# Instance norm on one core: gamma first on the ScalarE queue, its columns and the Sqrt table made while the first unit lands

## The chip, the cores and the metric

The kernel runs on one core of a Trainium2 chip. The metric is the time on the device in microseconds (us), the median of several executions. The profile is of one execution; its span is some 1.7 us shorter than the time that is reported for the same execution (625.1 us against 626.8 us before the change).

## The reference

```python
def reference(x, gamma):              # x: 4 x 8 x 16 x 256 x 256 float32, gamma: 8 x 16
    mu = x.mean(axis=(3, 4), keepdims=True)
    var = ((x - mu) ** 2).mean(axis=(3, 4), keepdims=True)
    x_norm = (x - mu) / np.sqrt(var + 1e-5)
    out = x_norm * gamma[None, :, :, None, None]
```

There are 512 channels of 65,536 numbers. Each channel is normalised by its own mean and variance and multiplied by its gamma. The input is 134.2 MB and so is the output; every byte has to be read once and written once.

## The kernel before

The kernel takes 16 channels at a time, a *unit*: 8 partitions for each channel, 8192 numbers (32 KB) in each partition, 4 MB in all. There are 32 units and six slots in SBUF. All six slots are filled at the start, so six loads (about 25 MB) are queued before any arithmetic is done. A later load waits until the store from its slot has landed.

```python
    g_row = singles.tile([1, G * C], F32, name="g_row")
    for u in range(AHEAD):                                   # AHEAD = 6
        load(u, nc.scalar if u in (1, 3) else nc.sync)
        if u == 1:
            nc.sync.dma_start(out=g_row[:], in_=gv[None, :])
    ...
    for u in range(U):                                       # U = 32
        t = slots[u % AHEAD]
        nc.vector.reduce_sum(out=st[:, u, 0:1], in_=t[:], axis=AX.X)
        square = nc.scalar.activation(out=junk[:], in_=t[:], func=ACTF.Square, accum_out=st[:, u, 1:2])
        ...
        if u == 0:
            gamma_columns()          # 8 matmuls spread gamma over the partitions, between two copies
        ps = psum.tile([P, 2], F32, name="ps")
        nc.tensor.matmul(out=ps[:], lhsT=navg_w, rhs=st[:, u], start=True, stop=True)
        # nvar on VectorE, std (Sqrt) on ScalarE, rstd and scale on VectorE   (cut)
        nc.vector.tensor_scalar(out=t[:], in0=t[:], scalar1=ps[:, 0:1], scalar2=scale[:, u : u + 1],
                                op0=ALU.add, op1=ALU.mult)
        nc.scalar.dma_start(out=ov[u], in_=t[:])
        if u + AHEAD < U:
            load(u + AHEAD, nc.sync)
```

So loads go out on the SyncE queue, stores and two of the first loads on the ScalarE queue. In the records these are the DMA queues q1 and q10.

## Time and profile before

| What | Before | Read from |
|---|---|---|
| Time | 626.93 us (626.88 to 627.35) | median of all runs |
| Span of the profiled execution | 625.1 us | the page |
| Bytes moved | 268.46 MB, 429 GB/s over the span | the page |
| VectorE, ScalarE, TensorE busy | 71%, 38%, 3% | the page |
| Unit 0 landed, first store issued | 22.6 us, 43.1 us | the timeline |

These are lines of the page of the kernel before: busy time in us (share of the span) and number of instructions, then busy tenths in 40 equal slices for VectorE, ScalarE and the 16 DMA engines, then GB/s in each slice.

```profile
PE 21.4 (3%) x80; PEld 19.5 (3%) x80; DVE 442.9 (71%) x162; ACT 239.9 (38%) x98; POOL 1.3 (0%) x9
DVE  0569999999898767867668676686766877667710
ACT  0435555544444423444224442244432444323400
DMA  8999999999999999999999999999999999999998
GB/s 371 434 436 419 419 436 436 436 436 436 435 436 435 428 426 436 426 436 436 434 436 436 434 434 432 428 432 426 436 436 434 436 436 434 434 436 428 428 436 359
```

The DMA row has a 9 in every slice but the first and the last, and the rate stays near 436 GB/s. No engine that computes is in that position. The Trainium skill ("DMA: Bandwidth & Descriptors", section "Specifications") gives a fabric ceiling of 435 GB/s, and this trace runs at it.

The timeline of the kernel before, cut to the first unit. The columns are start and duration in us, engine, line, operation, what it writes and reads, and in brackets the idle time before it with what ended it.

```profile
1.72 1.28 ACT L103 ACT_TABLE_LOAD   x1 [1.72 <-PEq L148]
22.61 8.69 DVE L102 TENSOR_REDUCE st<-xt 128x1 f32<-128x8192 f32 x1 [22.61 <-DMA xt<-in_x_dram]
31.21 0.67 DVE L78 COPY g_rep<-g_row 1x1024 f32<-1x1024 f32 x1
32.02 3.54 PE L83 MATMUL g_ps<-one,g_rep 1*128 1x1 f32 x16 [32.02 <-DVE g_rep L78]
36.12 0.29 DVE L114 TENSOR_SCALAR nvar<-ps 128x1 f32<-128x1 f32 x1 [0.36 <-PE ps L113]
36.49 1.28 ACT L118 ACT_TABLE_LOAD   x1 [6.76 <-DVE nvar L114]
38.51 4.55 DVE L127 TENSOR_SCALAR xt<-xt,ps,scale 128x8192 f32<-128x8192 f32 x1
43.09 0.35 ACTq L131 DMA_DIRECT2D out_dram<-xt  x1
```

Between the end of the first row sum (31.3 us) and the first store (43.1 us) stand gamma's columns (the copy, 16 matmul passes of 3.54 us in all, a copy back) and a load of the Sqrt table (1.28 us), the second table load of the kernel. VectorE waits for both. This is what the change goes after.

### The profile page before, as it was taken

The numbers are of one execution on the slowest core, as the hardware profiler recorded it, in microseconds if no ns is written. First come the engines' busy times: TensorE is split into PE (matmuls) and PEld (weight loads), VectorE is DVE, ScalarE is ACT, GpSimd is POOL, SyncE is SP. The second block draws the span as 40 slices with busy tenths as digits, with TensorE's granted clock in tenths as the row PEclk, the third lists the DMA queues.
The fourth block names the chain that finished last, engine by engine and source line by source line (L and its number), as shares of the span: only waits on it lengthen the run. The fifth ranks groups of instructions, "written<-read, shape, count | busy, mean of one in ns | idle before, by whom it ended". The sixth has DMA issues, their size and how long they took to land.

```text
span 625.1 us, 628 instructions
## 1 busy us (share of the span) xinstructions
PE 21.4 (3%) x80; PEld 19.5 (3%) x80; DVE 442.9 (71%) x162; ACT 239.9 (38%) x98; POOL 1.3 (0%) x9
## 2 busy tenths in 40 slices
PE   0020000000000000000000000000000000000000
PEld 0020000000000000000000000000000000000000
DVE  0569999999898767867668676686766877667710
ACT  0435555544444423444224442244432444323400
POOL 0000000000000000000000000000000000000000
DMA  8999999999999999999999999999999999999998
GB/s 371 434 436 419 419 436 436 436 436 436 435 436 435 428 426 436 426 436 436 434 436 436 434 434 432 428 432 426 436 436 434 436 436 434 434 436 428 428 436 359
DMA packets 9220, 268.46 MB, mean 429 GB/s; under 512 B 1025, under 2 KB 1026, under 8 KB 1026
## 3 DMA queue, kind: packets, MB, share of 16 engines
q10 hardware_dynamic: 4896, 142.61, 52.8%
q1 hardware_dynamic: 4322, 125.83, 46.8%
q14 instruction: 2, 0.02, 0.0%
HBM read 134.22 MB, written 134.22 MB: 429 GB/s over the span
## 4 chain that ended last, share of the span: by engine, by line
DMA 62%; DVE 30%; PE 2%; issue 1%; ACT 1%; SPq 0%; ACTq 0%
DMA xt<-in_x_dram 55%; DVE st L102 24%; DMA out_dram<-xt 7%; DVE xt L127 5%; PE ps L113 2%; DVE nvar L114 1%; PE g_ps L83 1%; ACT std L118 0%; ACT L118 0%; DVE rstd L122 0%; DVE scale L124 0%; DVE g_rep L78 0%; SPq L48 0%; ACTq L118 0%
## 5 line engine op out<-in xcount | busy, mean ns | idle before, releaser
L102 DVE TENSOR_REDUCE st<-xt 128x1 f32<-128x8192 f32 x32 | 277.9, 8684 | 110.2 <-DMA xt<-in_x_dram 110.2
L103 ACT ACTIVATE junk<-xt 128x8192 uint8<-128x8192 f32 x32 | 224.9, 7030 | 266.1 <-DMA xt<-in_x_dram 212.1
L127 DVE TENSOR_SCALAR xt<-xt,ps,scale 128x8192 f32<-128x8192 f32 x32 | 145.6, 4550 | 1.2
L118 ACT ACTIVATE std<-nvar,eps_t 128x1 f32<-128x1 f32 x32 | 9.4, 295 | 76.0 <-DVE nvar L114 76.0
L113 PE MATMUL ps<-st,navg 128*128 128x2 f32 x64 | 17.9, 349 | 536.4 <-DVE st L102 536.4
L113 PEld LDWEIGHTS ps<-st,navg 128*128 128x128 f32 x64 | 16.0, 311 | 538.2 <-issue 538.2
L114 DVE TENSOR_SCALAR nvar<-ps 128x1 f32<-128x1 f32 x32 | 9.2, 286 | 23.4 <-PE ps L113 23.4
L122 DVE RECIPROCAL rstd<-std 128x1 f32<-128x1 f32 x32 | 5.2, 164 | 12.9 <-ACT std L118 12.9
L103 ACT ACTIVATION_READ_ACCUMULATOR junk<-xt 128x1 f32 x32 | 6.0, 186 | 0.0
L124 DVE TENSOR_TENSOR scale<-rstd,g_col 128x1 f32<-128x1 f32 x32 | 5.1, 159 | 1.1
L83 PE MATMUL g_ps<-one,g_rep 1*128 1x1 f32 x16 | 3.5, 346 | 32.0 <-DVE g_rep L78 32.0
L83 PEld LDWEIGHTS g_ps<-one,g_rep 1*128 1x128 f32 x16 | 3.5, 325 | 32.0 <-issue 32.0
L118 ACT ACT_TABLE_LOAD x1 | 1.3, 1283 | 6.8 <-DVE nvar L114 6.8
L89 DVE COPY g_col<-g_ps 128x8 f32<-128x8 f32 x1 | 0.2, 166 | 3.7 <-PE g_ps L83 3.7
L103 ACT ACT_TABLE_LOAD x1 | 1.3, 1283 | 1.7 <-PEq L148 1.7
L78 DVE COPY g_rep<-g_row 1x1024 f32<-1x1024 f32 x1 | 0.7, 670 | 0.0
L64 POOL TENSOR_SCALAR_AFFINE_SELECT navg<-navg 128x128 f32<-128x128 f32 x1 | 0.4, 405 | 0.1
L68 POOL TENSOR_SCALAR_AFFINE_SELECT navg<-navg 128x128 f32<-128x128 f32 x1 | 0.4, 399 | 0.1
L63 POOL MEMSET navg<- 128x128 f32 x1 | 0.2, 222 | 0.0
L148 POOL MEMSET const-bfloat16-1.0<- 128x1 bf16 x1 | 0.1, 102 | 0.0
L148 POOL MEMSET const-uint8-127<- 128x1 uint8 x1 | 0.1, 102 | 0.0
L148 POOL MEMSET const-float32-0.0<- 128x1 f32 x1 | 0.1, 99 | 0.3 <-issue 0.3
(3 smaller groups left out, 0.3 us busy)
## 6 DMA issues: line engine op xcount, KB each, us to landing
out_dram<-xt ACTq DMA_DIRECT2D x32, 4096.0 KB, 64.1
xt<-in_x_dram SPq DMA_DIRECT2D x30, 4096.0 KB, 29.0
xt<-in_x_dram ACTq DMA_DIRECT2D x2, 4096.0 KB, 31.4
g_row<-in_gamma_dram SPq DMA_DIRECT2D x1, 0.5 KB
```

The costliest lines, as they stand in the source:

```text
L64: nc.gpsimd.affine_select(out=navg[:], in_=navg[:], pattern=[[-S, K], [0, S]], compare_op=ALU.is_ge, fill=0.0, base=0, channel_multiplier=1,)
L68: nc.gpsimd.affine_select(out=navg[:], in_=navg[:], pattern=[[S, K], [0, S]], compare_op=ALU.is_ge, fill=0.0, base=S - 1, channel_multipli ...
L78: nc.vector.tensor_copy(out=g_rep[:], in_=g_row[:].rearrange("o (n k) -> o n k", n=NG).unsqueeze(3).to_broadcast([1, NG, K, S]),)
L83: nc.tensor.matmul(out=g_ps[:, n : n + 1], lhsT=g_rep[:, n].rearrange("o k s -> o (k s)"), rhs=one[:], start=True, stop=True,)
L102: nc.vector.reduce_sum(out=st[:, u, 0:1], in_=t[:], axis=AX.X)
L103: square = nc.scalar.activation(out=junk[:], in_=t[:], func=ACTF.Square, accum_out=st[:, u, 1:2],)
L113: nc.tensor.matmul(out=ps[:], lhsT=navg_w, rhs=st[:, u], start=True, stop=True)
L114: nc.vector.tensor_scalar(out=nvar[:, u : u + 1], in0=ps[:, 0:1], scalar1=ps[:, 0:1], scalar2=ps[:, 1:2], op0=ALU.mult, op1=ALU.add,)
L118: nc.scalar.activation(out=std[:, u : u + 1], in_=nvar[:, u : u + 1], func=ACTF.Sqrt, bias=eps_t[:], scale=-1.0,)
L122: nc.vector.reciprocal(out=rstd[:, u : u + 1], in_=std[:, u : u + 1])
L124: nc.vector.tensor_mul(out=scale[:, u : u + 1], in0=rstd[:, u : u + 1], in1=g_col[:, g : g + 1],)
L127: nc.vector.tensor_scalar(out=t[:], in0=t[:], scalar1=ps[:, 0:1], scalar2=scale[:, u : u + 1], op0=ALU.add, op1=ALU.mult,)
```

## The change

Gamma's 512 bytes become the first transfer of the ScalarE queue, and the columns are made before unit 0 lands. A root of a small constant tile, which nothing uses, makes ScalarE load the Sqrt table at the start.

```diff
     for u in range(AHEAD):
+        if u == 1:
+            nc.scalar.dma_start(out=g_row[:], in_=gv[None, :])
         load(u, nc.scalar if u in (1, 3) else nc.sync)
-        if u == 1:
-            nc.sync.dma_start(out=g_row[:], in_=gv[None, :])
...
+    root_eps = singles.tile([P, 1], F32, name="root_eps")
+    nc.scalar.activation(out=root_eps[:], in_=eps_t[:], func=ACTF.Sqrt)
...
-    def gamma_columns():
-        (copy to g_rep, 8 matmuls to g_ps, copy to g_col)
+    (the same copy, 8 matmuls and copy, at once)
...
-        if u == 0:
-            gamma_columns()
```

More of the change, by code (lines that the diff above doesn't have):

```diff
@@ L75 @@
     g_col = singles.tile([P, NG], F32, name="g_col")
-    def gamma_columns():
-        nc.vector.tensor_copy(
-            out=g_rep[:],
-            in_=g_row[:].rearrange("o (n k) -> o n k", n=NG).unsqueeze(3).to_broadcast([1, NG, K, S]),
-        )
-        for n in range(NG):
-            nc.tensor.matmul(
-                out=g_ps[:, n : n + 1],
-                lhsT=g_rep[:, n].rearrange("o k s -> o (k s)"),
-                rhs=one[:],
-                start=True, stop=True,
-            )
-        nc.vector.tensor_copy(out=g_col[:], in_=g_ps[:])
+    nc.vector.tensor_copy(
+        out=g_rep[:],
+        in_=g_row[:].rearrange("o (n k) -> o n k", n=NG).unsqueeze(3).to_broadcast([1, NG, K, S]),
+    )
+    for n in range(NG):
+        nc.tensor.matmul(
+            out=g_ps[:, n : n + 1],
+            lhsT=g_rep[:, n].rearrange("o k s -> o (k s)"),
+            rhs=one[:],
+            start=True, stop=True,
+        )
+    nc.vector.tensor_copy(out=g_col[:], in_=g_ps[:])
     junk = singles.tile([P, F], U8, name="junk")
```

## The prediction

> **What bounds the kernel now.** The DMA engines do. The page's slice table has them at 9 tenths or more in every slice but the first and the last, moving about 436 GB/s; 268.46 MB at 436 GB/s is 616 us of the 625.1 us span. The Trainium skill, "DMA: Bandwidth & Descriptors", section "Specifications", gives a fabric ceiling of 435 GB/s; this trace agrees (436 GB/s in most slices). The trace's packet records sharpen this: 8192 packets of 32 KB, 1.213 us each, on 16 engines. The first starts at 2.1 us, the last ends at 623.9 us, and 512 packets per engine times 1.213 us is 621.1 us. So the engines lose about 0.7 us net, as slow packets in the first 5 us (up to 2.0 us each) and at 45 to 48 us, when the first store starts. VectorE is 71% busy, ScalarE 38%.
>
> **What the change does.** In the first unit's chain (view: the chain in order of time) it removes from between the end of the first row sum (31.29 us) and the first store's issue (43.09 us):
> - the gamma columns: from 31.29 to the mean-and-variance step at 36.12 us is 4.83 us now; in the second unit the same stretch (51.66 to 52.39) is 0.73 us. About 4.1 us go.
> - the second table load, 1.28 us. The Trainium skill, "ScalarE: Activation LUTs", "What ACT_TABLE_LOAD costs", says 1283 ns, as the trace does. No Square after the first root reloads, so Sqrt's set serves both: one load should remain.
>
> Added: one 128x1 root (0.3 us) on an idle ScalarE, and gamma's issue (0.3 to 0.45 us) before unit 1's load on the ScalarE queue. Unit 1's load starts about 0.4 us later; unit 0's may land up to one packet (1.2 us) sooner than 22.6 us.
>
> So the first store is issued about 5.4 us sooner, near 37.7 us (36.4 to 37.8), and VectorE's back-to-back units of 14.93 us follow as much earlier until DMA takes the pace (around 193 us before).
>
> **How much is on the critical path.** The view of the chain puts these steps on it, but they are hidden: during 31 to 43 us the DMA engines are full with the six loads queued in advance (six loads alone are about 58 us of DMA). The bytes and the rate stay. An earlier store only reorders them; what VectorE gains comes back as waiting later. Only slow packets can give something: at most 0.6 us at the first store and a few tenths at the start. I expect 0.4 us.
>
> **Predicted: 626.5 us**, 8 in 10 between 625.6 and 627.3. Faster by over 2%: 0.005; within 2%: 0.99; slower by over 2%: 0.005.
>
> **What would show it.** One table load of 1.28 us; g_rep and g_ps done before 15 us; first store issued near 37.7 us; loads of units 6 and on issued some us sooner; DMA rate still 436 GB/s, with the first packet near 2.1 us and the last ending 623 to 624 us; VectorE's and ScalarE's waits for loads grown by about 5 us each. Wrong if: the first store is issued later than 39 us; the table loads stay two; or the span falls by about 5 us, which would mean that the engines were not full.
>
> **What would make it wrong.** The queues could interleave otherwise at the end; the engine that carries gamma's packet could become the slowest of the 16 at the start; or a stretch without queued loads could open between 60 and 130 us. Each would cost or give a microsecond or two, not 2%.

## The result, and the profile after

| | Before | After |
|---|---|---|
| Time, median | 626.93 us (626.88 to 627.35) | 626.93 us (626.87 to 627.12) |
| Span | 625.1 us | 625.2 us |
| Unit 0 landed | 22.6 us | 20.3 us |
| First store issued | 43.1 us | 35.4 us |
| First packet of that store started | 48.2 us | 45.8 us |
| Last packet of the last load ended | 579.1 us | 581.5 us |
| Last packet of all ended | 623.91 us | 623.87 us |

The ratio is 0.9999 (95% interval 0.9982 to 1.0016). Ratios here are the mean time of one kernel's fast runs over that of the other's fast runs in the same rounds, so they are not quite the ratio of the medians quoted. The last three rows come from the trace's records of the single DMA packets.

The same page lines of the changed kernel:

```profile
PE 21.4 (3%) x80; PEld 19.5 (3%) x80; DVE 443.2 (71%) x162; ACT 238.8 (38%) x98; POOL 1.3 (0%) x9
DVE  0699999998867668676687766776667867668620
ACT  0444444444444224443244432344423443224400
DMA  8999999999999999999999999999999999999998
GB/s 369 436 417 424 434 436 436 436 436 437 434 436 434 426 426 430 434 436 436 436 434 434 436 434 434 430 426 430 434 436 436 436 432 434 436 436 434 426 426 365
```

And its timeline up to the first store, to be held against the lines of before:

```profile
2.06 0.68 DVE L79 COPY g_rep<-g_row 1x1024 f32<-1x1024 f32 x1 [2.06 <-DMA g_row<-in_gamma_dram]
2.24 1.28 ACT L74 ACT_TABLE_LOAD   x1 [2.24 <-issue]
2.88 3.54 PE L84 MATMUL g_ps<-one,g_rep 1*128 1x1 f32 x16 [2.88 <-DVE g_rep L79]
20.32 8.69 DVE L103 TENSOR_REDUCE st<-xt 128x1 f32<-128x8192 f32 x1 [13.70 <-DMA xt<-in_x_dram]
29.75 0.29 DVE L113 TENSOR_SCALAR nvar<-ps 128x1 f32<-128x1 f32 x1 [0.74 <-PE ps L112]
30.79 4.55 DVE L126 TENSOR_SCALAR xt<-xt,ps,scale 128x8192 f32<-128x8192 f32 x1
35.38 0.35 ACTq L130 DMA_DIRECT2D out_dram<-xt  x1
```

Everything that the change meant to do was done. The columns are ready by 7 us, there is one table load instead of two, and from landing to first store is 15.06 us instead of 20.48 us. The first store goes out 7.7 us sooner. Yet the DMA row is the same row of nines, and the last packet ends where it ended.

Where did the 7.7 us go? VectorE shows it. These are its row sums from the timelines around the place where it first has to wait for a load again, before and then after:

```profile
177.36 8.68 DVE L102 TENSOR_REDUCE st<-xt 128x1 f32<-128x8192 f32 x1
193.27 8.69 DVE L102 TENSOR_REDUCE st<-xt 128x1 f32<-128x8192 f32 x1 [0.89 <-DMA xt<-in_x_dram]
212.62 8.69 DVE L102 TENSOR_REDUCE st<-xt 128x1 f32<-128x8192 f32 x1 [4.33 <-DMA xt<-in_x_dram]
```

```profile
139.78 8.68 DVE L103 TENSOR_REDUCE st<-xt 128x1 f32<-128x8192 f32 x1
157.17 8.69 DVE L103 TENSOR_REDUCE st<-xt 128x1 f32<-128x8192 f32 x1 [2.36 <-DMA xt<-in_x_dram]
176.29 8.69 DVE L103 TENSOR_REDUCE st<-xt 128x1 f32<-128x8192 f32 x1 [4.10 <-DMA xt<-in_x_dram]
```

Back to back, a unit takes VectorE 14.93 us. The transfers allow one unit in 19.35 us (212.62 less 193.27). VectorE starts with a backlog of six loaded units and eats it up, and from then on it waits about 4.3 us in every unit. With an earlier start the backlog is eaten by 157 us instead of 193 us. Here are the waits of the kernel before and then of the changed kernel, with total us, number and longest:

```profile
DVE st L102 <- DMA xt<-in_x_dram: 110.2, 22, 22.6
```

```profile
DVE st L103 <- DMA xt<-in_x_dram: 111.2, 24, 13.7
```

In each, the longest wait is the one for unit 0. Without it VectorE waits 87.6 us for loads before and 97.5 us after. The 9.9 us of difference are, to within 0.2 us, the 7.7 us of the sooner first store and the 2.4 us by which the last load lands later. So the time was not saved and lost again by some new cost. It was turned from waiting at a place that held nothing up into waiting at another.

One caution on the chain of waits. It puts these steps on the chain that ended last, before the change too. For the changed kernel it puts 64% of the span down to "another core or an unknown queue", because it could not tell which transfer released which. A chain that passes through a step does not say that the step is worth its duration. The rate of the limiting resource says more.

### The profile page after: what moved, and what is told of

It is laid out like the page before. It is cut to its first block, busy times and chain, and to the rows that moved or that the text cites. A ratio compares the mean times of both kernels' runs of the same rounds, so it can differ in the third digit from the quotient of the medians.

```text
span 625.2 us, 626 instructions
## 1 busy us (share of the span) xinstructions
PE 21.4 (3%) x80; PEld 19.5 (3%) x80; DVE 443.2 (71%) x162; ACT 238.8 (38%) x98; POOL 1.3 (0%) x9
## 4 chain that ended last, share of the span: by engine, by line
another core or an unknown queue 64%; DMA 16%; DVE 13%; SPq 1%; PE 1%; issue 0%; ACT 0%
DMA xt<-in_x_dram 9%; DVE st L103 8%; DMA out_dram<-xt 7%; DVE xt L126 4%; SPq L48 1%; PE ps L112 1%; ACT std L117 0%; DVE nvar L113 0%; DVE rstd L121 0%; DVE scale L123 0%
## 5 line engine op out<-in xcount | busy, mean ns | idle before, releaser
L74 ACT ACT_TABLE_LOAD x1 | 1.3, 1283 | 2.2 <-issue 2.2
```

Of the source, the lines that this page charges most:

```text
L74: nc.scalar.activation(out=root_eps[:], in_=eps_t[:], func=ACTF.Sqrt)
```

## The experiments

The theory, called F in the expectations: the 16 DMA engines are full from the first packet at 2.1 us to the last at 624 us, so a shorter head changes nothing, and time is lost only where these engines have nothing to move. The rival, G: the head is on the critical path, as the chain of waits has it, and some other part of the change (unit 1's load, now behind gamma; the sooner store; the work on ScalarE) gives the gain back.

A measure used below is *missing engine time*. From the packet records, for every moment between the start of the first 32 KB packet and the end of the last, take how many of 16 packets are not in flight, add this up over time and divide by 16. It is 1.03 us before and 0.90 us after, in 621.8 us. *Slow packet time* is the excess of all packets' durations over 1.213 us (which is the usual one), summed and divided by 16: 1.32 us before, 1.41 us after.

### The parts one at a time: the table alone, gamma's load alone

```diff
# table alone: the kernel before, and
+    root_eps = singles.tile([P, 1], F32, name="root_eps")
+    nc.scalar.activation(out=root_eps[:], in_=eps_t[:], func=ACTF.Sqrt)
```

> The kernel before with the early root alone. Theory F (the 16 DMA engines are full from 2.1 us to 624 us, so the head of the compute chain is hidden): one table load instead of two, first store issued about 1.3 us sooner (43.09 to about 41.8 us), time within 0.2 us of the kernel before. Rival G (the head is on the critical path, and in the full change something else gives the gain back): about 1.3 us faster.

Measured: 626.95 us (before, on the same chip: 626.96 us), ratio 0.9998 (0.9983 to 1.0013). The first store was issued at 41.7 us, so the table load had cost the head 1.34 us of its 20.48 us, and the time did not move.

```diff
# gamma's load alone: the kernel before, and
     for u in range(AHEAD):
+        if u == 1:
+            nc.scalar.dma_start(out=g_row[:], in_=gv[None, :])
         load(u, nc.scalar if u in (1, 3) else nc.sync)
-        if u == 1:
-            nc.sync.dma_start(out=g_row[:], in_=gv[None, :])
```

> The kernel before with gamma's load moved to the front of the ScalarE queue and nothing else. It tells where the unexpected 2.3 us of unit 0's landing came from: if from the queue order, unit 0 lands at 20.3 us instead of 22.6 us and the first store is issued near 40.8 us; if from the early gamma work, it stays at 22.6 us. Theory F: time within 0.2 us of before. Rival G: 2.3 us faster, or slower if the later load of unit 1 is what gives the gain back.

Measured: 626.92 us, ratio 0.9998 (0.9983 to 1.0013). Unit 0 landed at 20.3 us and the first store went out at 40.8 us, both as expected from the queue order. The packet records show how: gamma's issue delays unit 1's load on the ScalarE queue by 0.57 us (1.37 less 0.80 in the changed kernel), but its first packet starts at 6.4 us instead of 3.8 us. By then each DMA engine has begun three packets of unit 0 and not one; two more turns of 1.213 us are 2.4 us. The engines then alternate between the queues packet by packet, as the Trainium skill says ("DMA: Bandwidth & Descriptors", section "Queues, rings and completion order"). So a small shift of issue became 2.3 us of landing, and it was worth nothing either. Neither part alone is faster or slower, so G's account, in which one part gains and another gives back, finds no support in either. The third part, making gamma's columns early, was not run alone; the run without arithmetic below covers it.

### A head shorter still: all first loads on the SyncE queue

```diff
# the changed kernel, and
-        load(u, nc.scalar if u in (1, 3) else nc.sync)
+        load(u, nc.sync)
```

> The changed kernel with all six first loads on the SyncE queue, gamma alone on the ScalarE queue, so unit 0 has the DMA engines to itself. Unit 0 should land near 13 us (8 packets per engine at 1.21 us instead of 14 to 16 turns) and the first store go out near 28 us, 15 us sooner than in the kernel before. Theory F: still within 0.3 us of before. Rival G: several us faster, as no load of unit 1 is delayed by gamma and the head is 15 us shorter.

Measured: unit 0 landed at 13.1 us and the first store was issued at 28.1 us, 15 us sooner than before the change. The time was 627.82 us (627.48 to 629.79), ratio 1.0021 (1.0002 to 1.0039). Shortening the head by another 7 us gained nothing; it was slower by 0.9 us, beyond the 0.3 us that F allowed. In the profiled execution the span is 0.9 us above that of the changed kernel, and the packet records have 0.54 us more missing and 0.57 us more slow time. Nearly all of the slow packets after the first few us lie between 29 and 75 us, after the issue of the first store. What makes them slow stayed open.

This run also shows a reverse side. The last load's last packet ended at 595.1 us instead of 579.1 us, and the last store was issued at 611.5 us instead of 595.5 us. Sooner stores take turns from the loads, so the loads end later. Not all of the 16 us is their doing, because here the SyncE queue carries all 32 loads and not 30; in the changed kernel, with 30, the last load ended at 581.5 us.

### No arithmetic at all: only the transfers

```diff
# the changed kernel, everything per unit left out but the transfers
     for u in range(U):
         t = slots[u % AHEAD]
-        (row sum, squares, mean and variance, root, scale, apply)
         nc.scalar.dma_start(out=ov[u], in_=t[:])
         if u + AHEAD < U:
             load(u + AHEAD, nc.sync)
```

> All arithmetic left out on purpose (the output is x, a wrong result): the same loads and stores through the same six slots, each store waiting for its load alone. Theory F: the transfers alone take as long as the whole kernel, 625.5 to 627 us. Rival G: clearly shorter, by 5 us or more, since no head chain is left.

Measured: 626.43 us (626.29 to 626.68), ratio 0.999 (0.9975 to 1.0005); the result is wrong, as intended. This is the strongest line against G. All the arithmetic of 32 units together costs 0.5 us beside its own transfers, and the interval of the ratio includes no difference at all. The engines' row on its page is the same row of nines:

```profile
DMA  8999999999999999999999999999999999999998
```

It also says what is left to win with this pattern of transfers: about 0.1%. No version was tried that beats both kernels, because this run leaves no room for one without other transfers.

### A head longer: extra row sums in unit 0

```diff
# the changed kernel, and, with N = 2, 3 and 5, after the first row sum
+        if u == 0:
+            for i in range(N):
+                nc.vector.reduce_sum(out=late[:, i : i + 1], in_=t[:], axis=AX.X)
```

> The changed kernel with 2 extra row sums (8.69 us each, results unused) in unit 0: first store issued near 35.4 + 17.4 = 52.8 us. Theory F: the six loads keep the engines busy until about 60 us, so the time stays within 0.3 us of before. Rival G: about 17 us slower than the changed kernel.

> 3 extra row sums: first store issued near 61.4 us, about 1.5 us after the six loads end (2.1 us + 6 x 8 packets x 1.213 us = 60.3 us), its first packet near 63.4 us. Theory F: the engines are empty for about 3 us and the time grows by 2 to 4 us. Rival G: 26 us slower.

> 5 extra row sums: first store issued near 78.8 us. Theory F: the engines are empty from about 60.3 us to 80.8 us and the time grows by about 20 us (18 to 23), less than half of the 43.4 us added. Rival G: 43 us slower.

| Extra sums | Head longer by, as issued | First store issued | Time | Missing engine time |
|---|---|---|---|---|
| 0 (the changed kernel) | 0 | 35.4 us | 626.93 us | 0.90 us |
| 2 | 16.6 us | 52.0 us | 627.29 us | 1.35 us |
| 3 | 25.0 us | 60.3 us | 630.21 us | 3.33 us |
| 5 | 42.1 us | 77.5 us | 647.24 us | 20.69 us |

The kernel before had 627.06 us on this chip; the ratios to it are 1.0006 (0.9991 to 1.0021), 1.005 (1.0035 to 1.0065) and 1.0325 (1.0308 to 1.0343). A head that is 16.6 us longer costs 0.2 to 0.4 us, depending on which of the two kernels it is held against. From there on a longer head is paid for: between 3 and 5 extra sums 17.1 us more head give 17.0 us more time. The bend lies where the six queued loads run out, near 60 us. The view by windows of the run with 5 extra sums shows the hole itself. The columns are the stretch, its length, busy time of PE, PEld, DVE, ACT and POOL (number of instructions), the clock, the DMA share and the GB/s.

```profile
56.00:60.00 4.00, 0.00 (x0) 0.00 (x0) 4.00 (x1) 0.00 (x0) 0.00 (x0) 1.00 1.08 467
60.00:64.00 4.00, 0.00 (x0) 0.00 (x0) 4.00 (x2) 0.00 (x0) 0.00 (x0) 1.00 0.00 0
64.00:68.00 4.00, 0.00 (x0) 0.00 (x0) 4.00 (x1) 0.00 (x0) 0.00 (x0) 1.00 0.00 0
68.00:72.00 4.00, 0.00 (x0) 0.00 (x0) 4.00 (x2) 0.00 (x0) 0.00 (x0) 1.00 0.00 0
72.00:76.00 4.00, 0.00 (x0) 0.00 (x0) 3.57 (x4) 0.29 (x1) 0.00 (x0) 1.00 0.00 0
76.00:80.00 4.00, 0.00 (x0) 0.00 (x0) 4.00 (x2) 2.14 (x1) 0.00 (x0) 1.00 0.62 262
```

Share and bytes of a packet are evidently counted in the window in which it starts: the packet records have the last load's packets ending at 61.4 us and the first store's starting at 78.6 us, 17.25 us in which the engines move nothing.

The accounts close: from the changed kernel to 5 extra sums the missing time grows by 19.8 us and the slow time by 0.7 us, and the span of the profiled executions by 20.3 us. The expected times were met by all three (within 0.3 us, 2 to 4 us, about 20 us); G's 17, 26 and 43 us were not. The stores were issued 0.8 to 1.3 us sooner than expected, and with 3 extra sums the right time was partly luck. There the first store started at 61.5 us and not at 63.4 us, so that only 0.35 us went missing where the six loads end. Most of the loss came later: with nothing else queued, the engines were wholly empty for 1.40 us from 71.4 us, between the end of the first store and the load that waited for it, and slow packets took 0.8 us more than in the changed kernel.

### The same change where the transfers do run dry: fewer slots

If F holds, the change must be worth something as soon as fewer loads are queued at the start. Both kernels were run with three slots and with four.

```diff
-    AHEAD = 6
+    AHEAD = 3        # and in the second pair: 4
```

> The kernel before with three slots instead of six (unit 3's load then waits for a store, and only unit 1 loads on the ScalarE queue). The three loads end near 31 us (2.1 us + 24 x 1.213 us), the first store goes out near 43 us. Theory F: the engines are empty for about 13 us, and the time is 12 to 18 us above the kernel before.

> The changed kernel with three slots: the first store goes out near 35.4 us, the engines are empty for about 6 us. Theory F: here the change is exposed, and this is about 7 us (5 to 9) faster than the kernel before with three slots. If instead the two three-slot kernels are within 1 us of each other, the gain is lost elsewhere than in full engines and theory F falls.

> The kernel before with four slots. The four loads end near 40.9 us (2.1 us + 32 x 1.213 us), the first store is issued near 43.1 us and its first packet starts near 44.3 us. Theory F (time is lost where the DMA engines have nothing to move): they are empty for about 3.4 us at the head, plus what four slots leave empty at the end.

> The changed kernel with four slots: the first store is issued near 35.4 us, before the four loads end, so the engines are not empty at the head. Theory F: faster than the kernel before with four slots by about 3.4 us (2 to 5), that is by the empty stretch at the head and not by the 7.7 us by which the first store is sooner. If it is 7 us or 0 us, counting empty DMA time at the head is not the right account.

| Slots | Before | After | Gain | Less missing engine time |
|---|---|---|---|---|
| 3 | 665.11 us (663.22 to 667.08) | 658.11 us (656.81 to 663.37) | 7.0 us | 27.02 to 20.01 us: 7.0 us |
| 4 | 633.59 us (632.79 to 634.42) | 629.16 us (629.01 to 629.23) | 4.4 us | 6.14 to 1.74 us: 4.4 us |
| 6 | 626.93 us | 626.93 us | 0.0 us | 1.03 to 0.90 us: 0.1 us |

The same edit is worth 7.0, 4.4 and 0.0 us. Here are the windows around the first store in the kernel before with four slots, and then in the changed kernel with four slots:

```profile
40.00:42.00 2.00, 0.00 (x0) 0.00 (x0) 2.00 (x1) 0.00 (x0) 0.00 (x0) 1.00 0.46 197
42.00:44.00 2.00, 0.00 (x0) 0.00 (x0) 2.00 (x2) 0.60 (x1) 0.00 (x0) 1.00 0.57 246
44.00:46.00 2.00, 0.00 (x0) 0.00 (x0) 2.00 (x1) 2.00 (x1) 0.00 (x0) 1.00 0.66 279
```

```profile
40.00:42.00 2.00, 0.00 (x0) 0.00 (x0) 2.00 (x1) 2.00 (x1) 0.00 (x0) 1.00 0.99 279
42.00:44.00 2.00, 0.00 (x0) 0.00 (x0) 2.00 (x1) 1.02 (x2) 0.00 (x0) 1.00 1.18 508
44.00:46.00 2.00, 0.56 (x2) 0.50 (x2) 0.82 (x5) 0.29 (x1) 0.00 (x0) 1.00 0.99 426
```

The last column of a window is GB/s and the one before it the DMA share. Before the change the share falls to about a half for two windows; after it, it does not. The packet records say it exactly: before, the engines are wholly empty for 2.38 us from 41.8 us and again for 1.40 us from 54.1 us, and after, at neither place. With three slots the empty stretches at the head are 12.05 and 1.37 us before, and 4.17 and 1.38 us after.

Not everything came as expected. The first hole with four slots is 2.4 us and not 3.4 us, and the second, while unit 4's load waits for the first store to land, was not foreseen. With three slots both kernels are far slower than the expected 12 to 18 us above the kernel with six slots (38 us before the change). The empty head was only part of that: both have another 10.2 us of empty engines before the last store, and slow packets that come back about every 60 us, where the ScalarE queue has run empty and a store starts again beside loads (11.45 and 14.48 us of slow time in all, against 1.32 us with six slots).

The table compares medians of several executions with the missing time of one, so that its exact agreement is partly luck. For the profiled executions alone the sum is this: with three slots 7.0 us less missing and 3.0 us more slow time, and 3.9 us between the spans (661.2 and 657.3 us); with four slots 4.4 us less missing and 1.0 us more slow time, and 3.4 us between the spans (630.9 and 627.5 us). In both pairs the profiled execution of the kernel before was the fastest of its four. That a gain appears and that it follows the empty head is shown; its size with three slots is known to some 3 us only.

## Why the prediction was right

- **What bounds the kernel.** Right. The transfers alone took 626.43 us, the kernel 626.93 us.
- **The costs in the head.** Right. The chain from landing to first store is 5.42 us shorter (20.48 to 15.06 us; predicted about 5.4 us), of which the table load is 1.34 us. The page shows one table load.
- **When the first store goes out.** Missed, in the harmless direction: 35.4 us, where 36.4 to 37.8 us was said. The step that was mis-sized is "unit 0's may land up to one packet (1.2 us) sooner". It landed 2.3 us sooner, since the later start of the other queue let two packets per engine pass and not one. The run with gamma's load alone showed that this comes from the queue order.
- **That the head is hidden.** Right, and tested both ways. A head 7.7 us shorter, 15 us shorter and 9 us longer than before all end within 0.9 us of it; a head that outlasts the queued loads is paid for in full; and with fewer queued loads the same edit gains.
- **"What VectorE gains comes back as waiting later."** Right in kind, too small in size: VectorE's waits for loads, without the first, grew by 9.9 us and not by about 5 us. The terms missing from the sum were unit 0's sooner landing (2.3 us) and the 2.4 us by which the last load comes later. ScalarE's waits, for loads and for VectorE together and without the first, grew by 9.1 us (246.5 to 255.6 us), where about 5 us was said of the loads alone; those, as the view splits them, grew by 19.9 us (192.5 to 212.4 us).
- **"I expect 0.4 us."** Nothing came. The prediction counted on slow packets at the first store going away. They moved with it: 0.64 us of slow time at 44 to 48 us before, and 0.62 us at 42 to 45 us after. In both kernels they are packets of loads, in the last 4 us or so before the first packet of the first store. The first packets of all were no better either (0.59 us before, 0.71 us after). The measured time lies 0.43 us above the predicted 626.5 us, inside the range.
- **Only part of the sooner issue reached the engines.** Not foreseen. The first store was issued 7.7 us sooner, but its first packet started 2.4 us sooner (48.2 to 45.8 us). Before the change, unit 3's load had left the ScalarE queue at 41.9 us, and the store started 5.1 us after its issue. After it, the store was issued at 35.4 us but stood behind unit 3's load in the same queue, whose last packet ended at 43.3 us, and started 2.6 us after that. With gamma's load alone the first store was issued at 40.8 us, and with no arithmetic at 20.4 us, and in both its first packet started at 45.8 us too. So in the new order of the queues the columns and the table load, the 5.4 us of the prediction, did not even let the store begin sooner. (In the old order the table load alone did, by 1.1 us, from 48.2 to 47.1 us, and that was worth nothing either.) Unit 6's load, which waits for this store, was issued only 2.3 us sooner (66.8 to 64.5 us).

## What to carry to other kernels

Before shortening a chain at the head of a kernel, ask what the limiting resource does in that stretch. If a queue of loads keeps it full, the chain is hidden up to the moment at which the queue runs dry (here about 60 us with six 4 MB loads), and its length is worth nothing up to there and all of it afterwards. The quickest proof is a copy of the kernel with all arithmetic left out; the second is to make the suspected chain longer and see where the time begins to rise. A chain of waits names steps that lie on a path, but not what their removal is worth.

## What the Trainium skill lacked or had wrong

- "ScalarE: Activation LUTs", section "What ACT_TABLE_LOAD costs", gives 1283 ns for the load and some 1380 ns of drain, 2.66 us for every switch. The load took 1283 ns here too. But no drain showed where ScalarE had been waiting: the load began at 36.49 us and the root at 37.79 us, and taking the load away shortened the head by 1.34 us.
- The same page, section "Table sets: the hidden batching unit", does not list Square among the functions that come with Sqrt. After the change one load serves 32 squares and 32 roots, with a correct result.
- "DMA: Bandwidth & Descriptors", section "Queues, rings and completion order", has the turns between queues packet by packet, as seen here. It does not say how much a small lead is worth: 0.57 us of later issue on one queue let every engine take two more packets of the other, 1.213 us each, and moved the other queue's 4 MB load 2.3 us forward.
- The same page does not say that a store waits longer to start behind queued loads of another queue than on empty engines. From issue to first packet took 4.6 us with only the SyncE queue full (all first loads on it), and 1.2 us on empty engines (5 extra sums).
- None of the pages read has the slow packets that the records show where the ScalarE queue has run empty and a store starts beside loads: in the two kernels with six slots once, some 25 packets of up to 1.9 us instead of 1.213 us, 0.6 us of all engines' time; with three slots about every 60 us, up to 2.8 us a packet. Their cause stayed open here.
